# Layer 1 attention: a new order of the loads that one head pair issues

## The chip, the cores and the metric

The kernel runs on one core of a Trainium2 chip. The metric is the device time of one launch in microseconds, as the median of several runs; less is better. A core has five engines with instruction streams of their own: TensorE (PE in the profile; PEld is its weight loads), VectorE (DVE), ScalarE (ACT), GpSimd (POOL) and SyncE (SP), which here does nothing but issue transfers between HBM and the on-chip memory. Sixteen DMA engines carry these out.

## What is computed

The whole program is a two-layer backbone over 2048 latent tokens on a grid of 32 x 64 and 256 context tokens. The change lies in the attention of layer 1. It has 16 heads of 64 features. Each latent token attends to a window of 8 x 16 grid neighbours with a learned bias, and to all 256 context tokens:

```python
def neighborhood_attention(q, k, v, k_ctx, v_ctx, rpb):
    ...
    s_lat = einsum('bqhd,brkhd->bhqrk', qr, kb) * scale + bias
    s_lat = where(col_mask, s_lat, -inf)
    s_ctx = einsum('bqhd,bchd->bhqc', qr, k_ctx) * scale
    p = softmax(concatenate([s_lat, s_ctx], -1))
    o = p[latent part] @ vb + p[context part] @ v_ctx
```

Everything is in float32. Layer 0 and the projections ahead of this stage are left out here; the output projection of layer 1 comes behind it.

## The kernel before

**One pair of heads at a time.** `odd_attention` (L1306) loops over eight pairs `j` (L1491). Scores are computed with the keys on the partitions and the queries along the free dimension. For a pair, `steps` (L1316) lists 20 steps, called s0 to s19 from here on. A step ("l", n) takes one block of 128 latent keys against the rectangle of queries that can reach them; a step ("c", n) takes the 256 context keys against 512 queries. The order is s0, s1 = c0, c1; s2 to s5 = l0 to l3; s6 = c2; s7 to s10 = l4 to l7; s11 = c3; s12 to s15 = l8 to l11; s16 to s19 = l12 to l15.

**A step.** For each of the two heads `scores` (L1372) issues two matmuls into a PSUM bank (`st`, four banks): L1373 takes the 128 rows of the first key tile, L1374 the 65 rows of the second. In a latent step DVE then adds the bias table out of PSUM (L1535) and ACT takes the exponential (L106, L1541); in a context step ACT takes the exponential straight from PSUM. The products with the values (L1385 and L1406, into banks `o`) and the sums of the exponentials (POOL, L1412, and DVE, L1396) follow some steps later: steps wait in `pend`, and when six are there, four are flushed (L1559). A finished block of 512 queries is normalised (L838, L843 to L845) and written to HBM from POOL's queue (L848).

**The tiles that are loaded.** All loads of the loop go through `load` (L108), which issues on SP and chains each load behind the one before, so that SP issues them in the order of the program's text. For a pair:

- `query(j, i)` (L1327), once for each head `i`: three loads of 64 x 2048 float32 (512 KB each) and a row of 8 KB. Tile `q`.
- `tables(j)` (L1362): two loads of 517 KB. Tile `tab`. `mask` (L1368) later adds a constant to them on POOL.
- `keys` (L1341): a chunk of 512 latent keys, `kt`, as two loads (512 KB for the first matmul, L1344, and 256 KB for the second, L1347); also the context keys, `kc` (256 and 128 KB).
- `values(j)` and `values_ctx(j)` (L1352, L1358): 1024 KB and 128 KB, tile `ov`.

Four key chunks serve a pair: chunk 0 for s2 to s5, chunk 1 for s7 to s10, chunk 2 for s12 to s15, chunk 3 for s16 to s19. There are **two buffers** for chunks (`kt1` and `kt2` twice each), so a chunk's load can start when the chunk two before it has been used for the last time.

**Where in a pair the loads are issued.** While pair `j` is computed, the tiles of pair `j + 1` are loaded (L1495 to L1508), in between the chunks of pair `j` itself (L1512). In program order: at s0 the queries of head 0 and the tables of the next pair; at s2 the queries of head 1 of the next pair, then chunk 1 of this pair; at s7 chunk 2; at s8 the values; at s10 the mask (POOL); at s12 chunk 3; at s13 the context keys; at s16 chunk 0 of the next pair. Chunk 1 of pair 0 is loaded ahead of the loop (L1465). In pair 7 there is no next pair; the output weights are loaded at odd steps in its place (L1509).

The scheduler of the framework orders the instructions of each engine at build time. Between the two kernels, the sequence of PE, DVE, ACT and POOL instructions is the same, row by row, in operation, tiles and shapes; only the order of SP's loads differs.

Of the kernel before, what the change touches and what calls it, by code (L numbers as in the profile page):

```python
# [61 lines left out]
def rect(kind, g, c):  # L62

    (r, nr), (k, nk) = reach(kind, 0, g), reach(kind, 1, c)
    while nr * nk < 256:
        k, nk = (k, nk + 1) if k == 0 else (k - 1, nk + 1)
    return (r, nr), (k, nk)


def even(a, n):  # L70

    b = a // 2 * 2
    return b, (a + n + 1) // 2 * 2 - b, a - b
# [15 lines left out]
class Kern:  # L89
# [1216 lines left out]
    def odd_attention(self, out, right, left, wout):  # L1306
# [4 lines left out]
        with ExitStack() as es:  # L1311
# [12 lines left out]
            def qtile(j, i, part):  # L1324
                return self.tl(qa if i == 0 else qb[j % 2], [P, SEQ], f"q{part}{i}", F32R, bufs=2 - i)

            def query(j, i):  # L1327

                b, q1, q2 = i * 64, qtile(j, i, 1), qtile(j, i, 2)
                for u in range(2):  # L1330
                    self.load(q1[u * 64 : u * 64 + 64].bitcast(F32), self.Q1[0, j, b : b + 64])
                self.load(q2[:64].bitcast(F32), self.Q1[1, j, b : b + 64])
                self.load(q2[64:65].bitcast(F32), self.M1[2 * j + i : 2 * j + i + 1])
                return q1, q2
# [6 lines left out]
            def keys(j, c0, w, pool, tag):  # L1341

                k1 = self.tl(pool, [P, 2, w], tag + "1", F32R, bufs=len(ones[tag]))
                self.load(k1[:].bitcast(F32), self.K1t[j, :, :, c0 : c0 + w].rearrange("i d t -> d i t"))  # L1344
                k2 = ones[tag].pop(0)
                ones[tag].append(k2)
                self.load(k2[:64].bitcast(F32), self.K1t[j, :, :64, c0 : c0 + w].rearrange("i d t -> d i t"))  # L1347
                return k1, k2

            chunk = lambda j, g: keys(j, CTX + g * 512, 512, kp, "kt")  # L1350

            def values(j):  # L1352
                V = self.tl(vp[j % 2], [P, NT, P], "ov", bufs=1)
                f, c = j // 4, slice(j % 4 * P, j % 4 * P + P)
                self.load(V[:, NCT:, :], self.V1[f].rearrange("(n p) d -> p n d", p=P)[:, :, c])
                return V

            def values_ctx(j, V):  # L1358
                f, c = j // 4, slice(j % 4 * P, j % 4 * P + P)
                self.load(V[:, :NCT, :], self.V1c[f, :, :, c])  # L1360

            def tables(j):  # L1362
                tabs = [self.tl(tp[j % 2], [P, NR, NC], f"tab{i}", bufs=1) for i in range(2)]
                for i, tb in enumerate(tabs):
                    self.load(tb[:], self.i["rpb_k"][2 * j + i].rearrange("p (r c) -> p r c", r=NR))
                return tabs

            def mask(tabs):  # L1368
                for tb in tabs:
                    nc.gpsimd.tensor_tensor(out=tb[:], in0=tb[:], in1=mk[:], op=ALU.add)  # L1370

            def scores(ps, k1, k2, q1, q2):  # L1372
                nc.tensor.matmul(ps, k1, q1, start=True, stop=False)  # L1373
                return nc.tensor.matmul(ps, k2, q2, start=False, stop=True)  # L1374
# [80 lines left out]
            def rows(tile, RT, o, ks):  # L1455
                self.load(tile[:, ks, :], RT[ks, :, o * P : o * P + P].rearrange("j p t -> p j t"))

            Q, kc, kt, V, tabs, raw = {}, {}, [], {}, {}, {}
            Q[0, 1] = query(0, 1)
            kt.append(chunk(0, 0))  # L1460
# [30 lines left out]
            for j in range(8):  # L1491
                OA[j] = {}, {}
                for s, (kind, n) in enumerate(steps):
                    g, c = divmod(n, 4)
                    if j < 7:  # L1495
                        if s == 0:
                            Q[j + 1, 0] = query(j + 1, 0)
                            tabs[j + 1] = tables(j + 1)
                        elif s == 2:
                            Q[j + 1, 1] = query(j + 1, 1)  # L1500
                        elif (kind, n) == ("l", 5):
                            V[j + 1] = values(j + 1)
                            values_ctx(j + 1, V[j + 1])
                        elif (kind, n) == ("l", 9):
                            kc[j + 1] = keys(j + 1, 0, CTX, kcp, "kc")
                        elif s == 10:
                            with self.tc.issue_after(self.psum.ins):
                                mask(tabs[j + 1])  # L1508
                    elif s % 2 and s < 16:  # L1509
                        next(out_w)  # L1510
                    pts = exps() if kind == "l" else [exps(), exps()]
                    if kind == "l" and c == 0 and (j, g) not in ((0, 0), (7, 3)):  # L1512
                        kt.append(chunk(j + (g == 3), (g + 1) % 4))
                    for i in range(2):
                        q1, q2 = Q[j, i]
                        if kind == "c":
                            for u in range(2):
                                ps = bank()
                                ks, qs = slice(u * P, u * P + P), slice(n * 512, n * 512 + 512)
                                mm = scores(ps[:], kc[j][0][:, i, ks], kc[j][1][:65, i, ks], q1[:, qs], q2[:65, qs])  # L1520
                                ex = self.act(pts[i][:, u, :], ps[:], AF.Exp)
                            continue
                        k1, k2 = (k[:, i, c * P : c * P + P] for k in kt[0])
                        (r0_, nr), (c0, w) = rect("k", g, c)
                        ps = bank()
                        a, m, d = even(c0, w)
                        pt = pts[:, i, : nr * w].rearrange("p (r c) -> p r c", r=nr)
                        ps = ps[:, : nr * m].rearrange("p (r c) -> p r c", r=nr)
                        q1, q2 = (q[:].rearrange("d (r c) -> d r c", r=32)[:, r0_ : r0_ + nr, a : a + m] for q in (q1, q2))
                        mm = scores(ps, k1, k2[:65], q1, q2[:65])  # L1530
                        ps = ps[:, :, d : d + w]
                        for ro, ri, rn in pieces("k", 0, g, r0_, nr):
                            for co, ci, cn in pieces("k", 1, c, c0, w):
                                d = slice(ro, ro + rn), slice(co, co + cn)
                                nc.vector.tensor_tensor(out=pt[:, d[0], d[1]], in0=ps[:, d[0], d[1]],  # L1535
                                                        in1=tabs[j][i][:, ri : ri + rn, ci : ci + cn], op=ALU.add)
                    if kind == "l" and c == 3:
                        kt.pop(0)
                    if kind == "l":
                        pts = pts[:, :, : nr * w]  # L1540
                        ex = self.act(pts, pts, AF.Exp)  # L1541
                        pts = pts.rearrange("p i (r c) -> p i r c", r=nr)
                    pend.append((tail_ctx if kind == "c" else tail, n, pts, j, V[j], *OA[j]))
                    if j == 7 and s > 3:
                        with self.tc.issue_after(ex.ins):
                            next(out_s, None)
                    if j == 7 and n == 11:
                        z0, r0 = [exps([P, KD, P]) for _ in range(2)]
                        rows(z0, self.z1, 0, all_k)
                        rows(r0, self.RT1, 0, most_k)  # L1550
                        nc.gpsimd.tensor_tensor(out=r0[:, most_k, :], in0=r0[:, most_k, :], in1=z0[:, most_k, :], op=ALU.mult)
                    elif j == 7 and n == 12:
                        x0 = exps([P, D])
                        self.load(x0[:], self.x1[CTX : CTX + P, :])
                        gate = ones["kt"][0][:].rearrange("p i c -> p (i c)").bitcast(F32)
                        self.load(gate, self.gates[1, 0:1].partition_broadcast(P))
                        hi0, lo0 = [exps([P, KD, P], F32R) for _ in range(2)]
                        self.project_split(r0[:, most_k, :], hi0[:, most_k, :], lo0[:, most_k, :])
                    if len(pend) == 6:  # L1559
                        with self.tc.issue_after(mm.ins):  # L1560
                            flush(4)
# [135 lines left out]
```

## Time and profile before

| what | value |
|---|---|
| median of 3 runs | 3742.54 us (3739.37 to 3745.3) |
| the profiled execution's own time | 3737.21 us |
| its span, first to last instruction | 3735.4 us |
| mean granted TensorE clock | 0.977 |
| PE busy | 3586.5 us (96%) |
| DVE / ACT / POOL busy | 2377.3 / 1438.4 / 1209.3 us |
| DMA, mean over the span | 137 GB/s |
| first score matmul of pairs 1, 2, 3 | 3155.79, 3210.06, 3260.68 us |
| of pairs 4, 5, 6, 7 | 3311.10, 3362.39, 3413.45, 3467.42 us |

The span is the time from the first to the last instruction of one profiled execution; its own time holds 1.8 us more around it. The median of the plain runs is 5.3 us above that execution. "Granted clock" is the share of full speed that the chip gave TensorE. A row of the timeline gives start, duration (merged where several alike follow each other), engine, line, operation and tiles, and in square brackets how long the engine was idle before it and who ended that. A row of the stretches gives, for a window A:B, its length, then for each engine the busy time and the count of instructions, the granted clock, the mean busy share of the 16 DMA engines and their rate. In this case a window is mostly bounded by the first score matmul of two steps.

### The profile page before, as it was taken

How to read it: one execution, taken by the hardware profiler on the slowest of the kernel's cores; microseconds unless marked ns; L12 is line 12 of the kernel's file. 1: busy time of each engine (PE TensorE's matmuls, PEld its weight loads, DVE VectorE, ACT ScalarE, POOL GpSimd, SP SyncE). 2: the span in 40 equal slices, each digit the busy share in tenths (PEclk: the TensorE clock that was granted, in tenths of full speed). 3: DMA queues.
4: the chain of work that ended last, by engine and by line, in shares of the span. 5: the costliest groups of instructions: out<-in, count | busy, mean ns of one | idle time of the engine just before them, and what ended most of it. 6: DMA issues, size and time to landing. Idle time of an engine off the chain costs nothing.

```text
span 3735.4 us, 51753 instructions
## 1 busy us (share of the span) xinstructions
PE 3586.5 (96%) x18404; PEld 2766.2 (74%) x18404; DVE 2377.3 (64%) x4860; ACT 1438.4 (39%) x2741; POOL 1209.3 (32%) x1336
## 2 busy tenths in 40 slices
PE   7999989999999999999999999999899999999889
PEld 6988987888886666655657878888688886555567
DVE  4677656888866666697654345545578774566722
ACT  4445541111125555545552134444322224444400
POOL 1434330001011222212202233333444435776643
PEclk9999999999999999999999999999999999999999
DMA  7455452222242241434515545445544438778464
GB/s 258 135 167 160 128 170 95 82 76 85 74 137 66 69 113 58 115 88 136 143 51 169 168 145 152 147 142 169 187 139 135 140 104 228 182 197 206 144 194 129
DMA packets 364371, 512.18 MB, mean 137 GB/s; under 512 B 25825, under 2 KB 243889, under 8 KB 358210
## 3 DMA queue, kind: packets, MB, share of 16 engines
q1 hardware_dynamic: 322642, 425.49, 39.1%
q0 software_dynamic: 19872, 55.92, 5.0%
q10 hardware_dynamic: 21600, 27.46, 2.1%
q8 instruction: 146, 2.39, 0.3%
q14 instruction: 111, 0.91, 0.1%
HBM read 329.38 MB, written 179.37 MB: 136 GB/s over the span
## 4 chain that ended last, share of the span: by engine, by line
PE 78%; DMA 9%; DVE 7%; ACT 2%; POOL 2%; issue 2%; SPq 0%; POOLq 0%; ACTq 0%; DVEq 0%
PE gm L129 9%; PE gm L130 9%; PE gm L131 9%; PE av L905 7%; PE st L963 4%; PE mx L651 4%; PE st L964 3%; PE st L965 3%; PE pj L129 3%; PE pj L130 3%; PE pj L131 3%; DMA kt<-K1t 2%; PE o L1406 2%; PE st L1373 2%; DMA wraw<-w_od 1%
## 5 line engine op out<-in xcount | busy, mean ns | idle before, releaser
L954 DVE TENSOR_TENSOR acc<-acc,apt 128x512 f32<-128x512 f32 x512 | 365.4, 738 | 155.9 <-ACT apt L106 153.0
L106 ACT ACTIVATE apt<-st 128x512 f32<-128x512 f32 (+1 forms) x592 | 344.6, 594 | 284.1 <-PE st L965 250.8
L652 DVE TENSOR_REDUCE mm<-mx 128x1 f32<-128x512 f32 (+1 forms) x656 | 389.2, 629 | 82.0 <-PE mx L651 75.0
L905 PE MATMUL av<-apt,av 128*64 128x512 f32 (+1 forms) x1184 | 287.6, 599 | 0.0
L963 PE MATMUL st<-aq,akh 97*128 97x512 f32 (+1 forms) x592 | 254.0, 429 | 5.1 <-ACT apt L106 2.7
L651 PE MATMUL mx<-mk,mq 96*128 96x512 f32 (+1 forms) x656 | 236.7, 373 | 6.3 <-DMA mq<-QT 4.7
L964 PE MATMUL st<-aq,akh 96*128 96x512 f32 (+1 forms) x592 | 235.3, 398 | 0.0
L965 PE MATMUL st<-aq,akl 96*128 96x512 f32 (+1 forms) x592 | 234.1, 396 | 0.0
L1286 DVE CUSTOM_DVE_ANT_1 mx<-mx,mtab 128x225 f32<-128x225 f32 (+12 forms) x576 | 183.8, 339 | 59.5 <-PE mx L1280 44.2
L1535 DVE TENSOR_TENSOR opt<-st,tab 128x64 f32<-128x64 f32 (+10 forms) x576 | 143.0, 316 | 115.5 <-PE st L1374 90.2
L106 ACT ACTIVATE u<-gm 128x352 f32<-128x352 f32 (+1 forms) x140 | 68.6, 497 | 371.0 <-PE gm L131 208.7
L905 PEld LDWEIGHTS av<-apt,av 128*64 128x64 f32 x1184 | 82.0, 138 | 156.8 <-issue 155.5
L963 PEld LDWEIGHTS st<-aq,akh 97*128 97x128 f32 x592 | 112.3, 190 | 98.0 <-issue 43.7
L1412 POOL TENSOR_TENSOR oacc<-oacc,opt 128x682 f32<-128x682 f32 (+9 forms) x144 | 169.5, 1200 | 28.0 <-ACT opt L106 26.9
L1073 POOL TENSOR_TENSOR px<-py,px 128x512 f32<-128x512 f32 x64 | 86.4, 1350 | 232.2 <-DVE py L1072 229.6
L106 ACT ACTIVATE opt<-opt 128x930 f32<-128x930 f32 (+8 forms) x130 | 104.4, 805 | 123.9 <-DVE opt L1535 115.1
L106 ACT ACTIVATE prh<-pr 128x1024 fp32r<-128x1024 f32 x32 | 33.9, 1058 | 263.0 <-PE pj L130 235.3
L651 PEld LDWEIGHTS mx<-mk,mq 96*128 96x128 f32 x656 | 121.7, 189 | 17.8 <-issue 5.1
L1373 PE MATMUL st<-q,kt 128*128 128x480 f32 (+5 forms) x256 | 104.4, 410 | 31.6 <-DVE opt L1535 15.9
L965 PEld LDWEIGHTS st<-aq,akl 96*128 96x128 f32 x592 | 113.7, 192 | 25.5
L964 PEld LDWEIGHTS st<-aq,akh 96*128 96x128 f32 x592 | 114.0, 193 | 18.1
L106 ACT ACTIVATE x<-px,modB,modA 128x128 f32<-128x128 f32 x272 | 99.3, 469 | 58.0 <-PE px L331 55.3
(517 smaller groups left out, 10097.4 us busy)
## 6 DMA issues: line engine op xcount, KB each, us to landing
q<-Q SPq DMA_DIRECT2D x48, 512.0 KB
H<-x ACTq DMA_DIRECT2D x36, 512.0 KB
adaw<-ada_w SPq DMA_DIRECT2D x64, 256.0 KB
x<-H SPq DMA_DIRECT2D x32, 512.0 KB
pr<-RT SPq DMA_DIRECT2D x32, 512.0 KB
wraw<-w_od SPq DMA_DIRECT2D x64, 256.0 KB
K1t<-okt POOLq DMA_DIRECT2D x32, 512.0 KB, 7.7
kt<-K1t SPq DMA_DIRECT2D x32, 512.0 KB
```

The lines of the kernel that those rows point to most:

```text
L106: return self.nc.scalar.activation(out, in_, func, **kw)
L129: self.nc.tensor.matmul(out, lh(k), rh(k), start=j == 0, stop=False)
L130: self.nc.tensor.matmul(out, lh(k), rl(k), start=False, stop=False)
L131: yield self.nc.tensor.matmul(out, ll(k), rh(k), start=False, stop=j == n - 1)
L651: mm = nc.tensor.matmul(ps[:, :w], q[:A_QK, (t % 6) * P : (t % 6) * P + P], k[:A_QK, k0 : k0 + w], start=True, stop=True)
L652: nc.vector.tensor_reduce(out=m[:, t, n : n + 1], in_=ps[:, :w], axis=AX.X, op=ALU.max)
L905: nc.tensor.matmul(O[j, nb][i * 64 : i * 64 + 64, :w], V[j, kt // TT][:, kt % TT, i * 64 : i * 64 + 64], pts[i][:, :w], start=n == 0, stop ...
L954: nc.vector.tensor_tensor(out=acc[i][:, :w], in0=a[:, :w], in1=pts[i][:, :w], op=ALU.add)
L963: nc.tensor.matmul(ps[:, :w], kh[: A_QK + 1, i, kq], qh[: A_QK + 1, :w], start=True, stop=False)
L964: nc.tensor.matmul(ps[:, :w], kh[:A_QK, i, kq], ql[:A_QK, :w], start=False, stop=False)
L965: mm = nc.tensor.matmul(ps[:, :w], kl[:A_QK, i, kq], qh[:A_QK, :w], start=False, stop=True)
L1286: nc.vector.tensor_tensor_reduce(out=s, in0=s, in1=tb[:, ri : ri + rn, ci : ci + cn], scale=1.0, scalar=-3e38, op0=ALU.add, op1=ALU.max, a ...
```

## The change

`CHUNK` names the step at which each chunk is loaded. Chunk 1 of the pair moves from behind both heads' queries and the tables (s2) to the head of the pair (s0). The next pair's queries of head 0 move from s0 to s1, the tables from s0 to s4, chunk 2 from s7 to s6, the queries of head 1 from s2 to s7, chunk 3 from s12 to s11, the values from s8 to s13, the context keys from s13 to s15. Chunk 0 of the next pair stays at s16, and the mask at s10.

```diff
+            CHUNK = {0: 1, 6: 2, 11: 3, 16: 0}
...
                     if j < 7:
-                        if s == 0:
+                        if s == 1:
                             Q[j + 1, 0] = query(j + 1, 0)
+                        elif s == 4:
                             tabs[j + 1] = tables(j + 1)
-                        elif s == 2:
+                        elif s == 7:
                             Q[j + 1, 1] = query(j + 1, 1)
-                        elif (kind, n) == ("l", 5):
+                        elif s == 13:
                             V[j + 1] = values(j + 1)
                             values_ctx(j + 1, V[j + 1])
-                        elif (kind, n) == ("l", 9):
+                        elif s == 15:
                             kc[j + 1] = keys(j + 1, 0, CTX, kcp, "kc")
...
-                    if kind == "l" and c == 0 and (j, g) not in ((0, 0), (7, 3)):
-                        kt.append(chunk(j + (g == 3), (g + 1) % 4))
+                    if s in CHUNK and (j, s) not in ((0, 0), (7, 16)):
+                        kt.append(chunk(j + (s == 16), CHUNK[s]))
```

On SP the order in one pair was: q (head 0), tab, q (head 1), kt 1, kt 2, ov, kt 3, kc, kt 0 of the next pair. It becomes: kt 1, q (head 0), tab, kt 2, q (head 1), kt 3, ov, kc, kt 0 of the next pair. Count and sizes of the loads stay the same.

## The prediction

> **What bounds the kernel now.** I begin with the page: the span, and the chain of work that ended last, by engine and by line.
>
> ```profile
> span 3735.4 us, 51753 instructions
> ...
> PE 78%; DMA 9%; DVE 7%; ACT 2%; POOL 2%; issue 2%; SPq 0%; POOLq 0%; ACTq 0%; DVEq 0%
> PE gm L129 9%; PE gm L130 9%; PE gm L131 9%; PE av L905 7%; PE st L963 4%; PE mx L651 4%; PE st L964 3%; PE st L965 3%; PE pj L129 3%; PE pj L130 3%; PE pj L131 3%; DMA kt<-K1t 2%; PE o L1406 2%; PE st L1373 2%; DMA wraw<-w_od 1%
> ```
>
> TensorE sets the end. The one load of the changed stage on the chain is the key chunk: 2% of the span, some 75 us. That is no price: the chain counts from a load's issue to its landing, and PE worked during most of it. What PE lost is in the view of PE's waits, taken over the eight pairs (total us, times, longest).
>
> ```profile
> PE st L1373 <- DVE opt L1535: 13.7, 26, 2.0
> PE st L1373 <- DMA kt<-K1t: 10.6, 5, 2.9
> PE st L1374 <- DMA kt<-K1t: 4.0, 6, 1.3
> ```
>
> PE stood still 10.6 + 4.0 = 14.6 us for key chunks. PE's timeline puts all of it at one place: s7, the first matmuls on chunk 1, in each of pairs 1 to 6. Pair 4 first, then the same place in pair 7, where chunk 1 came in time.
>
> ```profile
> 3334.61 0.64 PE L1373 MATMUL st<-q,kt 128*128 128x360 f32 x1 [2.49 <-DMA kt<-K1t]
> 3335.47 0.67 PE L1374 MATMUL st<-q,kt 65*128 65x360 f32 x1 [0.23 <-DMA kt<-K1t]
> ...
> 3336.54 0.60 PE L1373 MATMUL st<-q,kt 128*128 128x480 f32 x1
> ```
>
> ```profile
> 3489.14 0.39 PE L1373 MATMUL st<-q,kt 128*128 128x480 f32 x1
> ```
>
> The same 128x480 matmul takes 0.60 us behind the stall and 0.39 without it. So the stall has a second price, a lower clock. The stretches show both: from the first score matmul of s5 to that of s11, for pairs 1 to 7 in order.
>
> ```profile
> 3166.93:3192.41 25.48, 21.91 (x105) 11.94 (x106) 12.80 (x31) 9.33 (x14) 13.80 (x12) 0.80 0.83 203
> 3221.21:3243.02 21.81, 20.08 (x104) 11.11 (x105) 12.88 (x31) 9.37 (x14) 12.36 (x11) 0.84 0.97 238
> 3271.85:3293.43 21.58, 19.31 (x104) 9.67 (x105) 13.24 (x32) 9.33 (x14) 11.07 (x11) 0.92 0.94 240
> 3322.25:3344.71 22.46, 19.72 (x104) 11.32 (x105) 12.98 (x31) 9.38 (x14) 13.00 (x11) 0.85 0.90 236
> 3373.54:3395.78 22.24, 19.83 (x104) 11.42 (x105) 12.97 (x31) 9.36 (x14) 13.09 (x11) 0.85 0.91 235
> 3424.61:3449.75 25.14, 21.49 (x104) 11.69 (x105) 13.23 (x32) 9.33 (x14) 13.13 (x11) 0.80 0.85 208
> 3478.57:3496.31 17.74, 17.09 (x105) 9.34 (x106) 17.67 (x35) 11.17 (x19) 9.55 (x10) 1.00 0.56 176
> ```
>
> The six take 138.71 us together; pair 7, at clock 1.00, takes 17.74 for the same matmuls although DVE has more to do there (17.67 us busy against some 13). The next rows give the whole of pairs 1 to 6 and four spells of low clock.
>
> ```profile
> 3155.79:3467.44 311.65, 285.84 (x1826) 175.48 (x1825) 191.72 (x541) 153.51 (x241) 219.48 (x196) 0.93 0.76 195
> 3221.40:3224.80 3.40, 3.40 (x10) 1.35 (x11) 2.98 (x13) 1.79 (x3) 2.90 (x3) 0.50 1.06 228
> 3272.60:3276.00 3.40, 3.40 (x10) 1.04 (x11) 2.43 (x11) 1.51 (x3) 3.15 (x2) 0.50 1.03 217
> 3334.10:3340.90 6.80, 6.07 (x18) 4.35 (x20) 4.54 (x9) 1.94 (x3) 2.54 (x3) 0.50 1.12 314
> 3436.50:3446.70 10.20, 8.57 (x32) 5.62 (x34) 5.04 (x10) 2.77 (x3) 3.98 (x4) 0.50 0.89 220
> ```
>
> A spell at 0.50 begins with the stall of pair 4 and with that of pair 6, and lasts 6.80 and 10.20 us. In pairs 2 and 3 a spell of 3.40 us begins at s5, ahead of any missing chunk: the small DVE waits of s3 to s5 can set it off too.
>
> **Why the chunk is late.** SP's timeline of pair 1, then the DMA share and rate (last two columns) in four stretches of it.
>
> ```profile
> 3154.97 1.75 SPq L111 DMA_DIRECT2D q<-Q  x3
> ...
> 3157.32 0.83 SPq L111 DMA_DIRECT2D tab<-rpb_k  x2
> 3158.24 2.43 SPq L111 DMA_DIRECT2D q<-Q  x3
> ...
> 3165.12 5.04 SPq L111 DMA_DIRECT2D kt<-K1t  x4
> 3171.47 0.36 SPq L111 DMA_DIRECT2D ov<-V  x1
> 3173.90 9.90 SPq L111 DMA_DIRECT2D ov<-V1c  x1
> 3192.42 1.06 SPq L111 DMA_DIRECT2D kt<-K1t  x2
> 3193.53 1.22 SPq L111 DMA_DIRECT2D kc<-K1t  x2
> 3202.40 1.04 SPq L111 DMA_DIRECT2D kt<-K1t  x2
> ```
>
> ```profile
> 3156.00:3187.50 31.50, 26.97 (x142) 15.69 (x143) 22.81 (x57) 16.43 (x27) 16.48 (x17) 0.89 1.02 255
> 3187.50:3193.00 5.50, 5.50 (x33) 2.98 (x30) 0.74 (x3) 0.00 (x0) 5.50 (x3) 0.71 0.01 2
> 3198.20:3203.00 4.80, 4.80 (x37) 3.05 (x34) 1.47 (x4) 0.64 (x2) 4.80 (x7) 1.00 0.02 5
> 3203.00:3207.00 4.00, 3.93 (x50) 3.00 (x51) 2.73 (x16) 3.00 (x4) 4.00 (x5) 1.00 0.74 199
> ```
>
> Chunk 1 stands behind both heads' queries and the tables: 2 x 1.57 + 1.06 MB by the tiles' shapes, 4.2 MB ahead of its own 0.79, at 255 GB/s in a queue without a gap. That is some 20 us and then the chunk, against the 21 us that an undisturbed pair has before s7 (11.1 to s5 in pair 1, 9.9 from s5 to s7 in pair 7). Later in the pair the queue is empty twice (0.01 and 0.02), as chunks wait for a buffer. What is late is an order, not a rate.
>
> **The change, step by step.** No instruction of PE, DVE, ACT or POOL is added, removed or moved against its neighbours. All terms are landings. I count from s0 of an undisturbed pair, which I build from rows: the six pairs last 311.65, their s5 to s11 138.71, so the rest is 172.94, or 28.8 each; with 17.74 that makes 46.6 us (now 51.9).
>
> 1. *Chunk 1 to s0.* It needs the buffer of the last pair's chunk 3, free when s19's scores end. The queries at 3154.97 already waited for the end of those scores, so its issue is no later than theirs. The chunk issued at 3202.40 into an empty queue was through by 3207.00 (199 GB/s x 4.00 us = 0.8 MB, all of it), so a lone chunk takes 4.6 us. It lands near 4; s7 needs it at 21. The stall goes.
> 2. *Queries, tables, chunk 2.* The queue is then full: 1.57 + 1.06 + 0.79 MB. Queries and tables belong to the next pair; what asks for the tables first is the mask on POOL.
>
> ```profile
> 3187.06 4.73 POOL L1370 TENSOR_TENSOR tab<-tab,maskk 128x1034 f32<-128x1034 f32 x2
> ```
>
> It ran 31 us into pair 1, which is about 23 into the shorter pair. The tables land near 4 + 2.63 / 0.255 = 14 to 18, by how much the result writes take. Chunk 2 is free to load once s5's scores end, at 12, lands near 20, and is needed at s12, behind s11 (28.9). Cost: nothing.
> 3. *Queries of head 1, chunk 3.* All that stands ahead of chunk 3, with four result writes of 0.26 MB, is 6.85 MB: 27 us. Chunk 3's buffer comes free at s11, 28.9; it lands at 33.5; s16 needs it at 38.9 (3202.40 less 3192.41 behind s11). Slack 5.4. The queue's empty time shrinks, but is still there.
> 4. *Values and context keys behind chunk 3.* 1.18 + 0.39 MB: 6.2 us, so 39.7. The next s0 needs `kc` at 46.6: slack 6.9. `kc` is issued behind the load from V1c, which held SP for 9.90 us in pair 1, with much queued ahead of it. Less is queued now; if it held SP as long, `kc` would land near 45.5, slack 1.1. These are the two ends; I take 39.7, as the queue ahead is one chunk, not three loads.
> 5. *Chunk 0 of the next pair* stays at s16, lands near 44, and is needed behind s1 of the next pair, past 50. Pairs 0 and 7 do not change: in both, chunk 1 was in time already.
>
> So s5 to s11 falls from 138.71 to 6 x 17.74 = 106.4: **32.3 us less**. Of this 14.6 is the stall, 17.7 the clock and DVE waits. Then something comes back. [...] I keep two of six, 1.7 us each (3.40 at half clock): 3.4. **The sum is -28.9 us** (bounds: -32.3 with no spell, -22.1 with six). The profiled execution, 3737.2, becomes 3708.3. The median of the runs is 5.3 higher; against it I forecast 3742.5 - 28.9 = **3714**.
>
> [...]
>
> **The rivals.**
>
> *Only the idle time comes back.* If the low clock hung on DVE's small waits and not on the stall, 14.6 us would go and the spells stay: 3728. For it: the spells of pairs 2 and 3. Against it: the spell of pair 4 starts inside the stall, and pair 7 has none.
>
> *DVE takes the chunk's place.* Pair 3 had the shortest stall, yet took 21.58; without its 1.7 of clock it is 19.9, not 17.7. If 19.9 is what the four PSUM banks allow, the gain is 138.7 - 119.4 - 3.4 = 15.9: 3727. Against it: pair 7, with more DVE work, has 17.74.
>
> *Nothing changes.* The chunk still lands late, as its buffer comes free late, or other loads hold SP. Time 3742. Against it: step 1.
>
> *Slower.* The context keys now come last but one. If the V1c load holds SP longer than 9.90 us, PE stalls at each s0, on `kc`. From a hold of about 14 us (9.9, the slack of 1.1, and a stall of 2.7 like pair 4's, whose stretch is 4.7 over pair 7's; 28.9 / 6 is 4.8) the pair is no shorter than now. At a stall of 5 us with 6.8 us at half clock behind it, each of six pairs loses 8.4: 50.4 - 28.9 = 21.5 more, 3764.
>
> **How the numbers follow.** Forecast 0.64; idle time alone 0.10; DVE 0.14; nothing 0.06; slower 0.06. Faster by over 0.2% (7.5 us, about what a measurement of this kernel can tell from no change): 0.64 + 0.10 + 0.14 = 0.88; within it 0.06; slower 0.06. The range reaches from the bound without spells, less the runs' own spread below their median and a few us of luck with the clock (3705), to the two weaker gains, with 2 us over (3730); it leaves out the last two cases and some edges, under 0.2.
>
> **What would show it.** PE's waits for `kt` are gone, and no wait for `kc` or a later chunk has come. The stretch s5 to s11 is near 17.7 in pairs 1 to 6, and up to 1.7 more where a spell begins at s5; s11 to the next s0 keeps its length. In SP's timeline `kt` comes first in a pair, and the empty time ahead of chunk 3 is shorter. I am wrong if s7 still waits, if the wait for DVE at s8 grows past pair 7's, if a spell of low clock stays in each pair, or if s0 or s16 begins to wait for a load.

## The result, and the profile after

The changed kernel takes 3709.32 us (median of 5 runs, 3707.57 to 3712.28), against 3745.3 us for the kernel before (5 runs, 3739.37 to 3747.11): 36.0 us less, a ratio of 0.9906 with a 95% interval of 0.9892 to 0.9919. The forecast was 3714, 28.9 us less than a median of 3742.5. The profiled execution took 3709.59 us.

On the page after, the key chunk is no longer among the first entries of the chain of work that ended last.

```profile
span 3707.8 us, 51752 instructions
...
PE 79%; DVE 7%; DMA 6%; POOL 3%; ACT 3%; issue 2%; SPq 0%; POOLq 0%; ACTq 0%; DVEq 0%
PE gm L129 9%; PE gm L130 9%; PE gm L131 9%; PE av L905 7%; PE st L963 4%; PE mx L651 4%; PE st L964 3%; PE st L965 3%; PE pj L129 3%; PE pj L130 3%; PE pj L131 3%; PE o L1406 2%; PE st L1373 1%; DMA wraw<-w_od 1%; PE mx L1280 1%
```

All of PE's waits over the eight pairs, from 3100 to 3510 us, in the changed kernel (L1537 is L1535 of before):

```profile
PE st L1373 <- DVE opt L1537: 22.3, 33, 3.7
PE st L1373 <- DVE rc L844: 2.4, 1, 2.4
PE st L1373 <- ACT opt L106: 1.4, 8, 0.2
```

There is no wait for a load, neither for chunk 1 nor for another. The waits for DVE have grown a little: in pairs 1 to 6 they are 10.8 us, where the kernel before has 8.1. The stretches from s5 to s11, pairs 1 to 7, in the columns known from before:

```profile
3170.80:3189.03 18.23, 17.18 (x104) 9.43 (x105) 12.70 (x31) 9.33 (x14) 10.75 (x10) 1.00 0.82 244
3217.87:3235.08 17.21, 16.86 (x104) 9.38 (x105) 12.79 (x31) 9.38 (x14) 10.76 (x10) 1.00 0.94 261
3263.91:3282.48 18.57, 17.54 (x104) 9.30 (x105) 13.15 (x32) 9.32 (x14) 11.10 (x11) 1.00 0.86 239
3311.31:3328.51 17.20, 16.87 (x105) 9.41 (x106) 12.78 (x31) 9.35 (x14) 10.75 (x10) 1.00 0.88 262
3357.33:3376.08 18.75, 18.42 (x105) 9.86 (x105) 12.81 (x31) 9.37 (x14) 10.72 (x10) 0.91 0.80 237
3404.91:3425.11 20.20, 19.15 (x105) 9.78 (x106) 13.14 (x32) 9.32 (x14) 11.08 (x11) 0.92 0.75 220
3453.93:3471.66 17.73, 17.08 (x105) 9.32 (x106) 17.66 (x35) 11.15 (x19) 9.54 (x10) 1.00 0.57 178
```

Four of pairs 1 to 6 come down to about the length of pair 7, which is unchanged (17.74 before, 17.73 now). Only pairs 5 and 6, the two longest, have a lower clock. Their spells, and the six pairs as a whole:

```profile
3159.64:3442.77 283.13, 269.52 (x1825) 165.57 (x1825) 191.06 (x541) 153.51 (x241) 217.86 (x193) 0.99 0.80 213
3357.70:3361.10 3.40, 3.40 (x10) 1.27 (x10) 2.81 (x13) 1.79 (x3) 2.59 (x3) 0.50 1.00 395
3405.50:3408.90 3.40, 3.40 (x10) 1.27 (x12) 2.58 (x11) 1.66 (x3) 3.00 (x2) 0.50 1.02 405
```

The six pairs took 311.65 us and take 283.13: 28.5 less, at a clock of 0.99 in place of 0.93. All of it comes from s5 to s11 (138.71 to 110.16); the rest of the six pairs takes 172.97 us, where it took 172.94. SP's timeline of pair 1 shows the new order, and the stretches of the DMA engines below it how the queue fills.

```profile
3159.59 1.06 SPq L111 DMA_DIRECT2D kt<-K1t  x2
3160.70 1.87 SPq L111 DMA_DIRECT2D q<-Q  x3
...
3163.17 0.86 SPq L111 DMA_DIRECT2D tab<-rpb_k  x2
3171.72 1.10 SPq L111 DMA_DIRECT2D kt<-K1t  x2
3172.87 1.88 SPq L111 DMA_DIRECT2D q<-Q  x3
...
3189.06 1.09 SPq L111 DMA_DIRECT2D kt<-K1t  x2
3190.20 0.59 SPq L111 DMA_DIRECT2D ov<-V  x1
3190.84 3.74 SPq L111 DMA_DIRECT2D ov<-V1c  x1
3194.63 1.82 SPq L111 DMA_DIRECT2D kc<-K1t  x2
```

```profile
3160.50:3187.00 26.50, 24.48 (x148) 13.83 (x148) 22.08 (x54) 15.68 (x26) 15.72 (x15) 1.00 0.96 259
3187.00:3189.80 2.80, 2.80 (x24) 2.11 (x21) 0.90 (x4) 0.24 (x2) 2.80 (x2) 1.00 0.00 0
3189.80:3195.00 5.20, 4.94 (x40) 3.46 (x40) 2.56 (x7) 4.10 (x7) 5.20 (x4) 1.00 0.94 238
3195.00:3201.50 6.50, 6.43 (x48) 4.03 (x44) 3.31 (x15) 2.08 (x3) 6.50 (x8) 1.00 0.89 224
```

The queue runs empty near 3186 (the share is 0.99 from 3160.5 to 3186.0 and 0.00 from 3187.0), some 26 us after s0 of pair 1 (3159.64). It stays empty to 3189.8, while chunk 3 waits for its buffer. Then it is busy until the context keys are in, by 3200.0 (the share is 0.18 from 3199 to 3200), and once more for chunk 0 of the next pair.

### The profile page after: what moved, and what is told of

Read it like the earlier page. It is cut to its first block, busy times and chain, and to the rows that moved or that the text cites. A ratio compares the mean times of both kernels' runs of the same rounds, so it can differ in the third digit from the quotient of the medians.

```text
span 3707.8 us, 51752 instructions
## 1 busy us (share of the span) xinstructions
PE 3566.3 (96%) x18404; PEld 2754.6 (74%) x18404; DVE 2374.2 (64%) x4860; ACT 1438.5 (39%) x2741; POOL 1209.2 (33%) x1336
## 4 chain that ended last, share of the span: by engine, by line
PE 79%; DVE 7%; DMA 6%; POOL 3%; ACT 3%; issue 2%; SPq 0%; POOLq 0%; ACTq 0%; DVEq 0%
PE gm L129 9%; PE gm L130 9%; PE gm L131 9%; PE av L905 7%; PE st L963 4%; PE mx L651 4%; PE st L964 3%; PE st L965 3%; PE pj L129 3%; PE pj L130 3%; PE pj L131 3%; PE o L1406 2%; PE st L1373 1%; DMA wraw<-w_od 1%; PE mx L1280 1%
## 5 line engine op out<-in xcount | busy, mean ns | idle before, releaser
L1537 DVE TENSOR_TENSOR opt<-st,tab 128x64 f32<-128x64 f32 (+10 forms) x576 | 142.7, 316 | 86.6 <-PE st L1374 58.3
```

## The experiments

The runs were made in three sets, each on one chip, with the kernel before timed beside them: 3747.25 us beside r1 to r4, 3741.46 beside r5 to r8, 3747.15 beside r9 to r11. The theory is that of the prediction: PE lost time only because chunk 1 landed after s7 was due, and lost it twice, as idle time and as a low clock. It has three rivals: the new order of the other loads carries a part of the gain; the low clock has another cause; loads share the engines, so that order in the queue matters little.

### Chunk 1 alone, and all but chunk 1

r1 takes the kernel before and moves one thing:

```diff
+                    if s == 0 and j > 0:
+                        kt.append(chunk(j, 1))
...
-                    if kind == "l" and c == 0 and (j, g) not in ((0, 0), (7, 3)):
+                    if kind == "l" and c == 0 and g > 0 and (j, g) != (7, 3):
```

> The old order of all loads, but chunk 1 goes to the head of the pair; queries, tables, values and context keys keep their old order among themselves. My theory: the whole cost was that chunk 1 stood behind 4.2 MB, so this does all that the change did: 3709 (3705 to 3713), the stretch s5 to s11 near 17.7 us in pairs 1 to 6, no wait of PE for kt. Rival, the spread of the other loads carries a part of the gain: 3718 to 3735, with a new wait for kt 2, kt 3 or kc in some pairs.

It took 3714.22 us, a ratio of 0.9916 (0.9903 to 0.993): 1.2 us above the expected range, but below the rival's. No wait for a load is left, and pairs 1 to 6 take 284.47 us in its profile.

r2 is the complement. In the changed kernel `CHUNK = {7: 1, 8: 2, 11: 3, 16: 0}` puts chunk 1 behind both heads' queries and the tables again.

> The other half: chunk 1 stays behind the queries of both heads and the tables, and all else is as in the change (values behind chunk 3, context keys behind the values). Two pairs of score matmuls of one pair change places on PE. My theory: s7 waits as before, some 14 us in all, and the low clock follows it: 3741 to 3748. Rival, the spread carries a part: 3715 to 3735.

It took 3749.02 us, a ratio of 1.0006 (0.9995 to 1.0017), 1 us above the expected range. Its waits for chunks:

```profile
PE st L1373 <- DMA kt<-K1t: 17.8, 7, 3.3
PE st L1374 <- DMA kt<-K1t: 4.3, 6, 0.9
```

One of the seven, 2.49 us, belongs to pair 7, where chunk 1 now stood behind the output weights. The others make 19.6 us in pairs 1 to 6, a little more than in the kernel before, and these pairs take 317.44 us. So the one move does all that can be measured, and without it the spread of the rest brings nothing. As r1 came out some us above the first measurement of the change, both were timed again on one chip.

> The changed kernel, beside chunk 1 alone on the same chip. My theory: both do the same; the two medians lie within 5 us of each other. Rival, the new order of the other loads is worth some us more: this one is 5 us or more below.

> Chunk 1 alone at the head of the pair, as before, beside the changed kernel on the same chip. My theory: within 5 us of the changed kernel. Rival: 5 us or more above it.

The changed kernel took 3716.03 us (ratio 0.9918, 0.9903 to 0.9933), chunk 1 alone 3712.46 (0.991, 0.9895 to 0.9925). They do the same, and the rival falls. The profile of chunk 1 alone has one wait for a chunk this time, of 0.7 us at s12 of pair 4; the changed kernel's has none.

### Chunk 1 in time, but not first

`CHUNK = {4: 1, 6: 2, 11: 3, 16: 0}` in the changed kernel: chunk 1 is then issued at s4, behind the tables and the queries of one head instead of two.

> The changed kernel, but chunk 1 stands behind the queries of head 0 and the tables, 2.63 MB, and ahead of chunk 2. My theory, a matter of landing before s7: 2.63 + 0.79 MB at 255 GB/s and some 3 us from issue to the end of the first transfer, so it lands near 16 us from s0, s7 needs it at 21: the same time as the change, 3709 (3705 to 3713), no wait for kt 1. Rival, chunk 1 has to be first: waits of 1 us and more at s7 and spells of low clock, 3718 to 3735.

It took 3716.38 us, a ratio of 0.9915 (0.9902 to 0.9929), with no wait for a load. That is 3 us above the expected range, but the changed kernel itself stood at 3716.03 in its second timing. Chunk 1 need not be first, only before s7.

### More ahead of chunk 1

r5 is the kernel before with `V[j + 1] = values(j + 1)` and `values_ctx` moved from s8 to s2, ahead of chunk 1.

> The kernel before, with the values (1.18 MB) moved ahead of chunk 1 as well: 5.4 MB ahead of it in place of 4.2. My theory, lateness by bytes: chunk 1 lands 4.6 us later (1.18 MB at 255 GB/s), so s7 waits 4.6 us more in each of pairs 1 to 6: 28 us more, and with longer spells of low clock in the pairs that had short ones, 28 to 45 more: 3770 to 3790. Rival, loads share the engines and do not queue in order, so more load ahead changes little: 3745 to 3755.

It took 3779.26 us, a ratio of 1.0101 (1.0084 to 1.0119), 37.8 us more. Its waits for chunks, over pairs 0 to 6, and pair 2's spell of low clock:

```profile
PE st L1373 <- DMA kt<-K1t: 43.3, 7, 7.7
PE st L1374 <- DMA kt<-K1t: 6.0, 7, 1.2
```

```profile
3245.60:3259.25 13.65, 9.24 (x34) 6.11 (x36) 4.54 (x9) 2.77 (x3) 5.72 (x4) 0.50 0.43 124
```

Without pair 0's 1.9 us, the waits at s7 rose from 14.6 to 47.4, or 5.5 us a pair for 1.18 MB; 4.6 was expected. The V1c load held SP for 9.82 us in pair 2, but the DMA engines had no gap in that time (their share was 1.07 from 3230 to 3235 and 1.00 from 3235 to 3240), so the hold is not what made the chunk late. They moved 203 GB/s in the second of these stretches, not 255; at that rate 1.18 MB takes 5.8 us by estimate, near the 5.5. So the 1.18 MB put ahead of the late chunk was paid in full, and the rival falls.

### Work in the stall

r4 leaves the loads as before and fills the stall with matmuls whose result is thrown away:

```diff
+                        if n == 4 and i == 0 and 0 < j < 7:
+                            for _ in range(8):
+                                nc.tensor.matmul(full, kc[j][0][:, 0, :P], Q[j, 0][0][:, :512], start=True, stop=True)
                         mm = scores(ps, k1, k2[:65], q1, q2[:65])
```

> The kernel before, with 8 more matmuls of 128x512 (1.9 us at full clock) ahead of s7 in pairs 1 to 6, on tiles that are there, into the bank that s7 then overwrites: work that is thrown away, so that TensorE is busy while chunk 1 is on its way. Some score matmuls change places. Chunk 1 lands no earlier. My theory, the stall sets off the low clock: idle time left at s7 falls under 1 us in most pairs, the spells behind s7 go, and what they cost comes back although 48 matmuls were added: 8 to 13 us faster than before (3732 to 3738). Rival, the low clock does not hang on the stall: the spells stay and the time is that of before or 1 to 3 us more.

It took 3732.96 us, a ratio of 0.9958 (0.9945 to 0.997), 14.3 us faster with 48 matmuls more. Its waits for chunks, then the place in pair 1:

```profile
PE st L1374 <- DMA kt<-K1t: 3.6, 3, 1.5
PE st L1373 <- DMA kt<-K1t: 2.4, 3, 0.9
```

```profile
3183.06 2.02 PE L1533 MATMUL st<-q,kc 128*128 128x512 f32 x8
3185.65 0.43 PE L1373 MATMUL st<-q,kt 128*128 128x360 f32 x1 [0.57 <-DMA kt<-K1t]
3187.57 0.44 PE L1374 MATMUL st<-q,kt 65*128 65x360 f32 x1 [1.49 <-DMA kt<-K1t]
...
3188.17 0.39 PE L1373 MATMUL st<-q,kt 128*128 128x480 f32 x1
```

The 128x480 behind the gap takes 0.39 us, not 0.60: no spell followed these two gaps, of 0.57 and 1.49 us behind the filler. Of the six pairs one, pair 5, still has a spell at s7, of 3.4 us; three others have one of 3.4 us at s5. Pairs 1 to 6:

```profile
3162.18:3462.32 300.14, 284.30 (x1873) 176.06 (x1873) 192.29 (x541) 153.53 (x241) 217.84 (x194) 0.98 0.78 203
```

The load order is that of the kernel before, PE still waits for chunk 1 in three pairs, and yet the clock is 0.98. Six undisturbed pairs are 279.4 (6 x 46.6); with the 6.0 us of waits and 11.2 of filler (48 matmuls that start 0.234 us apart) that is 296.6, so 3.5 is left for the clock and DVE, where 17.7 was before. The low clock behind s7 did hang on the idle time, and the rival falls.

### Where the margin ends

r6 issues the next pair's context keys behind its chunk 0, as the last load of a pair; r9 issues them only at s0 of the pair that needs them. The diff is that of r6 against the changed kernel; in r9 the two added lines stand under `s == 0`, with `j` in place of `j + 1`:

```diff
-                        elif s == 15:
-                            kc[j + 1] = keys(j + 1, 0, CTX, kcp, "kc")
...
                         kt.append(chunk(j + (s == 16), CHUNK[s]))
+                        if s == 16:
+                            kc[j + 1] = keys(j + 1, 0, CTX, kcp, "kc")
```

> The changed kernel, with the context keys of the next pair behind chunk 0 of the next pair, so issued at s16 and the last of all. This takes the slack of step 4. Chunk 0 is issued some 39.4 us after s0 and alone takes 4.6; the context keys, 0.39 MB, end 1.5 to 2 behind it, near 46; the next s0 comes at 46 to 47. My theory: no wait or one under 1 us at s0: 3709 to 3716. Rival, the price of lateness at s0 is that of s7: waits of 2 us and more at s0 with spells of low clock, 3725 and more.

It took 3709.71 us, a ratio of 0.9915 (0.99 to 0.993), with no wait for a load. The slack of step 4 was real.

> The changed kernel, but a pair's context keys are issued at s0 of the pair itself, behind chunk 1, for pairs 1 to 7. Chunk 1 waits for s19's last scores, lands 4.6 us after that, and the context keys 1.5 to 2 behind it; s0 needs them at once. Some score matmuls change places. This is the place of the fourth rival, with its price: a wait of 5 to 6 us at each of seven s0, and a spell of low clock of 7 to 10 us behind it that costs 3.4 to 5 more: 8.4 to 11 us for each pair, 59 to 77 us over the changed kernel: 3768 to 3787. Rival, the low clock costs nothing here because s0 and s1 leave PE time to spare: 35 to 42 over it: 3744 to 3752.

It took 3788.28 us, a ratio of 1.0116 (1.01 to 1.0133): 72.3 us over the changed kernel on the same chip, so slower than before by 41, and 1.3 us above the upper end of what was expected. The timeline of PE at pair 2's first matmuls, and then the stretch of the spell behind them:

```profile
3224.30 2.05 PE L1373 MATMUL st<-q,kc 128*128 128x512 f32 x4 [6.69 <-DMA kc<-K1t]
```

```profile
3219.30:3232.95 13.65, 8.65 (x30) 6.44 (x32) 5.58 (x6) 5.02 (x9) 5.03 (x5) 0.50 1.04 267
```

The waits are 6.3 to 6.9 us at s0 of each of seven pairs, 46.2 in all (for three of them the profile names no releaser). The rest, 26 us or 3.7 a pair, is put down to the low clock behind them. This is what the prediction's fourth rival would have looked like, at the price that it gave: 8.4 a pair for a stall of 5, 10.3 for 6.6.

### Both kernels once more

> The kernel before once more, for a second profile: waits for kt at s7 of pairs 1 to 6, some 12 to 18 us in all; the spells of low clock at s5 may fall on other pairs. 3737 to 3747.

> The changed kernel once more, for a second profile: no wait for kt in pairs 1 to 6, no spell of low clock at s7; the spells at s5 may fall on other pairs than 5 and 6. 3706 to 3713.

They took 3747.71 and 3702.89 us in one execution each: the first 0.7 us above its range, the second 3 us below it. Pairs 1 to 6 in the kernel before, then in the changed one, then in the changed one as profiled in r10:

```profile
3163.24:3477.99 314.75, 287.33 (x1825) 176.82 (x1825) 191.68 (x541) 153.54 (x241) 219.43 (x196) 0.92 0.75 193
```

```profile
3152.84:3435.98 283.14, 269.46 (x1826) 165.79 (x1825) 191.06 (x541) 153.41 (x241) 217.81 (x194) 0.99 0.80 213
```

```profile
3163.35:3449.80 286.45, 272.93 (x1826) 166.43 (x1825) 191.05 (x541) 153.48 (x241) 217.78 (x193) 0.98 0.79 210
```

The changed pairs repeat to 0.01 us in the first two profiles, with spells at s5 in pairs 5 and 6 again. In r10 they take 3.3 us more, with spells at s5 in pairs 2, 3, 5 and 6: two more, at some 1.6 us each. The pairs of before took 311.65 and 314.75 us, with waits for chunks of 14.6 and 16.4 us; in the second profile pair 5 has no such wait.

## Why the prediction was right, step by step

**What bounds.** The reading held: the chain's 2% for the key chunk was no price, the 14.6 us of waits and the clock behind them were. Its sum for the late chunk is loose: 4.2 MB at 255 GB/s are 16.5 us and the chunk 3.1 more, not 20 and then the chunk. PE got the two parts of the chunk 23 and 25 us after s0 of pair 1; three result writes of 0.26 MB in between, 3.1 us at that rate, are most of what the sum leaves out. r4 shows the second part apart from the first.

**Steps 1 and 2.** Chunk 1 to s0: shown by r1, r2 and r3. It is the whole gain, and what counts is landing before s7. The mask ran 27 us into pair 1 (23 was forecast) and did not wait for the tables. That the other loads cost nothing where they now stand was also right; that they bring nothing either was implied by pricing every other step at zero, and is shown by r2.

**Step 3.** The queue was through with all ahead of chunk 3 after some 26 us (forecast 27), and chunk 3 was issued 29.4 us after s0 (28.9). There was no wait at s16.

**Step 4.** Of the two ends for the V1c load the near one was right: it held SP for 3.74 us, not 9.90. From 3189.80 to 3200.00 the engines moved 232 GB/s x 10.2 us, or 2.37 MB, which is chunk 3, the values and the context keys (2.36 MB): these are in by 40.4 us after s0, where 39.7 was taken. The next s0 came at 47.1. The slack was 6.7 us (forecast 6.9), and r6 shows that it is not spent even by another 0.79 MB ahead.

**The sum.** s5 to s11 of six pairs: forecast 106.4 and 3.4 for two spells, 109.8; measured 110.16 (18.23 + 17.21 + 18.57 + 17.20 + 18.75 + 20.20). The rest of the six pairs kept its length, as forecast (172.94 and 172.97). Two of six pairs had the spell at s5, as forecast. What decides which pairs have it, no run shows: it was pairs 2 and 3 before, 5 and 6 after, and 2, 3, 5 and 6 in r10, the same kernel. So that it was two was luck. The parts are a little different: a quiet pair is 17.2, half a us under pair 7, and pairs 1, 3 and 6 wait about 1 us for DVE at s9, more than pairs 2 and 4 (18.23 and 18.57 against 17.21 and 17.20 at full clock). The rival that DVE takes the chunk's place had that much in it, but not the 19.9 a pair that it needed; 0.68 us of that figure was pair 3's own wait for the chunk.

**What the sum left out.** In the first pair of profiles s5 to s11 gives 28.55 us, the forecast's 28.9 almost to the number. By the second pair of profiles the six pairs gain 314.75 - 283.14 = 31.6, and with r10's 286.45 against the 311.65 they would gain 25.2, so a hit to 0.4 us is partly luck. The medians differ by 36.0 us, and 28.9 lies below the interval of that measurement (30.3 to 40.4 by the ratio). Timed again in r10, the change is worth 31.1 us, with an interval of 25.1 to 36.3 that holds 28.9. What goes beyond the six pairs was not traced to the change. Executions differ outside them anyway: the first score matmul of pair 0, where the changed stage begins, came at 3111.07 and 3119.04 us in the two profiles of the kernel before, and at 3113.92, 3108.06 and 3116.96 in those of the changed one. In the first pair of profiles the part from pair 7 to the end went from 268.0 to 265.0 us, but runs with the same attention have 265.3 (r11) and 268.7 (r10) there. So the difference between 36.0 and what the six pairs give stays unexplained.

**The rivals.** That nothing changes and that the kernel gets slower did not happen. That only the idle time comes back (3728) is excluded by the time and by r4, that DVE takes the chunk's place (3727) by the time and by the stretches of 17.2 to 18.6 us at full clock. The longest gap at s7 in the kernel before is 2.88 us, and five of its six stalls were met by a spell at 0.50; the 28.5 us that the six pairs gained are about twice the 14.6 us of waits.

## What to carry to other kernels

Look for the same stretch of work somewhere in the trace where the suspected load came in time: pair 7's 17.74 us said what the six other pairs were worth better than the waits or the chain did. Where a queue pays for the bytes ahead of a load as this one did (1.18 MB more ahead, 5.5 us later, in r5), give each load a landing time from those bytes and compare it with the time of its first use; move the one load that misses, and leave the rest alone. In this kernel a late load cost more than TensorE's idle time: without the 14.6 us of waits the six pairs were 28.5 us shorter, and the 46.2 us of waits in r9 made the kernel 72.3 us longer.

## What the runs showed of the hardware

At s7 the low clock came with the stall in five of six pairs of the kernel before (its first profile). The rows give the waits of PE for a load, and the time at a clock of 0.50 that began there (in pair 2 of the kernel before 0.4 us behind the second wait):

| profile | pair, step | waits, us | time at 0.50, us |
|---|---|---|---|
| kernel before | 1, s7 | 2.26 + 1.26 | 10.20 |
| kernel before | 2, s7 | 1.10 + 0.63 | 3.40 |
| kernel before | 3, s7 | 0.68 | none |
| kernel before | 4, s7 | 2.49 + 0.23 | 6.80 |
| kernel before | 5, s7 | 1.88 + 0.51 | 6.80 |
| kernel before | 6, s7 | 2.88 + 0.72 | 10.20 |
| r5 | 2, s7 | 7.59 + 0.40 | 13.65 |
| r9 | 2, s0 | 6.69 | 13.65 |
| r4 (filler ahead) | 1, s7 | 0.57 + 1.49 | none |

Pairs 1 and 6 of the kernel before had the same time at 0.50, though PE was busy for 9.97 us of the one and 8.57 us of the other.

In the first profiles of both kernels the waits ahead of s5 were the same in pairs 1 to 6, 0.28 and 0.52 us for DVE. A spell of 3.40 us began there in pairs 2 and 3 of the kernel before (at 3221.40 and 3272.60, 0.2 and 0.8 us behind the first score matmul of s5) and in pairs 5 and 6 of the changed one (at 3357.70 and 3405.50, 0.4 and 0.6 us behind it), and none in the other pairs.

SP was held at the load from V1c for 8.54 to 9.90 us in pairs 1 to 6 of the kernel before, where two chunks and the values were issued just ahead of it, and for 3.22 to 4.62 us in the changed one, where one chunk and the values were.
